# One 512-column run for both halves of the tokens in the projections of a two-block kernel

## The chip, the cores and the metric

One core of a Trainium2 chip runs the whole program. The metric is device time in microseconds (us), the median of several executions; lower is better. The engines are named as in the profile: PE (TensorE, with PEld for its weight loads), DVE (VectorE), ACT (ScalarE), POOL (GpSimd) and SP, which issues the transfers of the weights. PSUM is the memory into which PE accumulates; a tile of 128 x 512 fp32 values fills one of its banks.

## What is computed

A block with two layers runs first, then a second block, on 256 tokens of width 1024. The change touches only the first block:

```python
for l in range(DEPTH):                       # DEPTH = 2
    x = layer_norm(ALPHA * x + 0.5 * swiglu(x, ffn_w1[l, 0], ffn_w2[l, 0]), ...)
    x = layer_norm(ALPHA * x + hybrid_mixer(x, ...), ...)
    x = layer_norm(ALPHA * x + 0.5 * swiglu(x, ffn_w1[l, 1], ffn_w2[l, 1]), ...)

def swiglu(x, w1, w2):                       # D_FF = 2816
    g, u = jnp.split(x @ w1, 2, axis=-1)
    return (jax.nn.silu(g) * u) @ w2

def hybrid_mixer(x, w_in, ...):
    b_gate, c_gate, v, x_r, y_r, g_logits = jnp.split(x @ w_in, SPLITS, axis=-1)
    y_a = (b_gate * causal_depthwise_conv(c_gate * v, sc_w, 3)) @ w_out_conv
    xc = causal_depthwise_conv(x_r, rc_w, 4) + rc_b
    gates = sigmoid(per-head products of xc with rg_w)
    h = rg_lru(xc, gates[0], gates[1], a_param)          # a scan over the tokens
    y_b = (h * jax.nn.gelu(y_r)) @ w_out_rnn
    g_a, g_b = jnp.split(sigmoid(g_logits + b_merge), 2, axis=-1)
    return (g_a * y_a + g_b * y_b) @ w_o
```

## The kernel before

All products run on PE with fp32r operands, and the fp32 precision is kept by splitting each operand into a high part (rounded to fp32r) and a low part (the rest). A product is then three matmuls: high weight with high token, high weight with low token, low weight with high token.

**Weights.** `Weights` streams all weights in a fixed order as blocks of 1 MB; half of a block (128 x 1024) is the unit here, and it is called a weight half. `pump` splits a weight half: ACT casts it to the high part (L195), DVE subtracts that from the raw values for the low part (L196). Six split halves are held, so splits run some five halves ahead of PE. Every engine runs its instructions in the order in which the program wrote them, so where `pump`, `done` or `spend` stand in the code sets what ACT and DVE have ahead of them.

**Projections with the weights stationary.** `ws` (L314) takes one weight half, with 8 slices of 128 x 128, and for each slice k loads the high weights twice and the low weights once; each load is followed by a run of 256 columns (L317 with the high tokens, L318 with the low tokens, L319 again with the high tokens). All add into the same 256 columns of a PSUM tile. `group` does this for two halves and so fills one tile of 512 columns. The tokens are in `xT`, `za` or `hg`, laid out as [high/low, k, token].

**PSUM.** `mm_tile` hands out four tiles in turn (two of the pool `mm`, two of `mmo`). A tile can be written again only when those who read it are done: four tiles later.

**The feed-forward network** (`ffn`). The first two of 22 pairs of weight halves are done in another form (`begin`, `finish`, L334). Then 20 calls of `pair(p)`: two halves of w1 in `group`, SiLU by ACT (L534), the product with the other half by DVE (L536), the split of the result `ht` (L311 by ACT, L312 by DVE). In the first pair `turn_early` transposes the results of the first two halves and splits them into `ht` as well. After pair p (up to p = 18) the down projection `ts` runs for pair p - 2 (L370: twelve matmuls of 512 columns); it reads the split `ht` of that pair.

**The mixer** (`mixer`). Two groups of four slices each. In a group: projections Y and X in pairs of halves (Gelu by ACT, convolution by DVE, L649 and L651), then for each of four slices C and V (`c_gate * v` on DVE, L723, its convolution L725 and L727), the recurrent gates (L666 to L668), and per two slices two halves B, whose product with the convolution (L741) is split into `za` (L311, L312). The steps of the recurrence (`lru`, L678 to L703) are pieces that `done` puts between the others; they end with `hg`. Then eight steps of the output: two halves of gate logits (`gs`, L766), one half `woc` that reads all of `za`, one half `wor` that reads all of `hg` (in `merge`), and the down projection `wo`. After each stage a layer norm follows (`tail`, `ln_vec`, `to_xT`).

The rest of the kernel, from 1297 us on, is the second block; its own projections still go through `ws`.

Of the kernel before, what the change touches and what calls it, by code (L numbers as in the profile page):

```python
# [9 lines left out]
F32 = mybir.dt.float32  # L10
# [214 lines left out]
def kernel(ctx, tc, x, blocks, vecs, lnrows, consts, rows, bias_w, wr, out):  # L225
# [88 lines left out]
    def ws(ps, half, xT, mid=None):  # L314
        w = half.rearrange("p h (k c) -> p h k c", k=8)
        for k in range(8):
# [3 lines left out]
            if mid and k == 3:  # L320
                mid()

    def group(keys, xT, then=None, mid=None):
        ps = mm_tile()
        for q, key in enumerate(keys):
            half = W.take(*key)
            ws(ps[:, q * 256:q * 256 + 256], half, xT, mid)
            (then or done)()
        return ps
# [41 lines left out]
                                 start=(first and hx == 0 and hw == 0), stop=(last and hx == 1))  # L371

    def new_xT():
        return apool.tile([128, 2, 8, 256], F32R, tag="xT", name="xT")

    def to_xT(xT, src, T, new=mm_tile, mid=None):
        todo = []
# [130 lines left out]
    def ffn(l, j, xT, last):  # L508
# [12 lines left out]
        def pair(p):  # L521
            turn = [0]

            def then():
                W.release()
                turn[0] += 1
                if turn[0] == 1:
                    W.pump(1)
                    if p == 2:
                        turn_early()  # L530

            ps = group([("w1", l, j, p, 0), ("w1", l, j, p, 1)], xT, then)
            sl = p1.tile([128, 512], F32, tag="t512", bufs=3, name="sl")
            nc.scalar.activation(sl[:, 0:256], ps[:, 0:256], AF.Silu)  # L534
            h32 = p1.tile([128, 256], F32, tag="t256", bufs=4, name="h32")
            nc.vector.scalar_tensor_tensor(h32, ps[:, 256:512], 0.5, sl[:, 0:256], op0=ALU.mult, op1=ALU.mult)  # L536
            W.pump(1)
            ht = p1.tile([128, 2, 256], F32R, tag="h2k", bufs=8, name="ht")
            split_out(ht[:, 0], ht[:, 1], h32)
            hs[p] = ht  # L540
            c = ada_block(l, j, p)
            if c is not None:
                if p == 6:
                    nc.scalar.activation(cb, cb, AF.Silu)
                w = W.take("ada", c)
                nc.vector.scalar_tensor_tensor(junk, w, 1.0, cb, op0=ALU.mult, op1=ALU.mult, accum_out=modc[:, c:c + 1])
                W.release_raw()
            step(1.2)
# [49 lines left out]
    def mixer(l, xT):  # L598
        v0 = l * V_LAYER

        def col(o):
            return vec[:, v0 + o:v0 + o + 1]
# [17 lines left out]
                    nc.tensor.transpose(pts[i // 2][:, o:o + 128], ev[T][:, i * 128:i * 128 + 128], ident)  # L620
            return pts

        za = p1.tile([128, 2, 8, 256], F32R, tag="za", name="za")
        hg = p1.tile([128, 2, 8, 256], F32R, tag="hg", name="hg")
        for grp in range(2):
            b = 4 * grp
            gely = p1.tile([128, 4, 256], F32, tag="gely", name="gely")
# [3 lines left out]
            aa = p1.tile([128, 4, 256], F32, tag="grp4", name="aa")  # L631
            xch = {}
            for i in (0, 2):
                if b + i == 0:
                    ps, px = early()
                else:
                    ps = group([("in", l, OFF_YR, b + i + q) for q in range(2)], xT)
                nc.scalar.activation(gely[:, i:i + 2].rearrange("p a t -> p (a t)"), ps, AF.Gelu_apprx_tanh)
                ps = px if b + i == 0 else group([("in", l, OFF_XR, b + i + q) for q in range(2)], xT)
                xps = []  # L640
                for q in range(2):
                    xp = p1.tile([128, 260], F32, tag="xp", bufs=2, name="xp")
                    nc.vector.memset(xp[:, 0:3], 0.0)
                    nc.scalar.copy(xp[:, 3:259], ps[:, q * 256:q * 256 + 256])
                    xps.append(xp)
                for q in range(2):
                    f = b + i + q
                    xp, o = xps[q], xc[:, i + q]
                    nc.vector.tensor_scalar(o, xp[:, 0:256], col(V_RC + f), col(V_RCB + f), op0=ALU.mult, op1=ALU.add)  # L649
                    for t in range(1, 4):  # L650
                        nc.vector.scalar_tensor_tensor(o, xp[:, t:t + 256], col(V_RC + 8 * t + f), o, op0=ALU.mult, op1=ALU.add)  # L651
                    xh = p1.tile([128, 2, 256], F32R, tag="h2k", bufs=8, name="xch")
                    soon.append(lambda xh=xh, o=o: split_out(xh[:, 0], xh[:, 1], o))
                    xch[i + q] = xh
# [53 lines left out]
            for i in (0, 2):  # L708
                pcs = []
                for q in range(2):  # L710
                    f = b + i + q
                    ps = mm_tile()
                    h = W.take("in", l, OFF_C, f)
                    ws(ps[:, 0:256], h, xT)
                    done(1)
                    h = W.take("in", l, OFF_V, f)
                    ws(ps[:, 256:512], h, xT)
                    done(1)
                    cs = p1.tile([128, 256], F32, tag="t256", bufs=4, name="cs")
                    nc.scalar.copy(cs, ps[:, 0:256])  # L720
                    pc = p1.tile([128, 260], F32, tag="xp", bufs=2, name="pc")
                    nc.vector.memset(pc[:, 0:2], 0.0)
                    nc.vector.tensor_mul(pc[:, 2:258], ps[:, 256:512], cs)  # L723
                    cv = p1.tile([128, 256], F32, tag="t256", bufs=4, name="cv")
                    nc.vector.tensor_scalar(cv, pc[:, 0:256], col(V_SC + f), None, op0=ALU.mult)  # L725
                    for t in range(1, 3):
# [2 lines left out]
                    for hd in range(2):  # L729
                        if GATES[hd] == i + q:  # L730
                            gates(hd)
                            if hd:
                                bg.append(lru())
                ps = mm_tile()
                for q in range(2):
                    h = W.take("in", l, OFF_B, b + i + q)
                    ws(ps[:, q * 256:q * 256 + 256], h, xT)
                    done(1)
                for q in range(2):
                    f = b + i + q  # L740
                    nc.vector.tensor_mul(pcs[q], ps[:, q * 256:q * 256 + 256], pcs[q])  # L741
                    split_out(za[:, 0, f], za[:, 1, f], pcs[q])
        acc = new_acc()
        g = []
# [2 lines left out]
        held = {}  # L747

        def merge(i):
            ps, gs = held.pop(i)  # L750
            h = W.take("wor", l, i)
            ws(ps[:, 256:512], h, hg)
            done(1)
            m2 = p1.tile([128, 512], F32, tag="t512", bufs=3, name="m2")
            nc.vector.tensor_mul(m2, ps, gs)
            m1 = p1.tile([128, 256], F32, tag="t256", bufs=4, name="m1")
            nc.vector.tensor_add(m1, m2[:, 0:256], m2[:, 256:512])
            mt = p1.tile([128, 2, 256], F32R, tag="h2k", bufs=8, name="mt")
            split_out(mt[:, 0], mt[:, 1], m1)
            ms[i] = mt  # L760

        for i in range(8):
            ps = group([("in", l, OFF_G, 8 * q + i) for q in range(2)], xT)
            gs = p1.tile([128, 512], F32, tag="gs", bufs=2, name="gs")
            for q in range(2):
                nc.scalar.activation(gs[:, q * 256:q * 256 + 256], ps[:, q * 256:q * 256 + 256], AF.Sigmoid,  # L766
                                     bias=col(V_BM + 8 * q + i), scale=1.0)
            ps = mm_tile()
            h = W.take("woc", l, i)
            ws(ps[:, 0:256], h, za)  # L770
            done(1)
            held[i] = ps, gs
            if i == 1:
                flush()
            if i >= 1:
# [1022 lines left out]
```

## Time and profile before

| | us |
|---|---|
| median of 3 runs | 1801.39 (1798.95 to 1804.64) |
| the profiled execution | 1805.13 |
| its span, first to last instruction | 1803.3 |
| granted TensorE clock, mean | 0.984 |

| engine | busy us | share of the span |
|---|---|---|
| PE | 1741.4 | 97% |
| PEld | 1580.5 | 88% |
| DVE | 1286.3 | 71% |
| ACT | 975.8 | 54% |
| POOL | 62.1 | 3% |

By time: first feed-forward network to 212 us, first mixer to 459, second network to 652, third to 843, second mixer to 1090, fourth network to 1297, second block to the end. A busy PE in this profile is one whose runs overlap (a run of 256 columns is listed with 283 ns, while the next one starts 120 ns after it), so rates are to be read from the starts of the instructions and not from their lengths. The same holds in a smaller measure for DVE and ACT, whose listed times include a last part under which the next instruction already runs. The clock in the views is the share of full speed: 1.00 is 2.4 GHz, 0.50 is 1.2 GHz.

### The profile page before, as it was taken

How to read it: one execution, taken by the hardware profiler on the slowest of the kernel's cores; microseconds unless marked ns; L12 is line 12 of the kernel's file. 1: busy time of each engine (PE TensorE's matmuls, PEld its weight loads, DVE VectorE, ACT ScalarE, POOL GpSimd, SP SyncE). 2: the span in 40 equal slices, each digit the busy share in tenths (PEclk: the TensorE clock that was granted, in tenths of full speed). 3: DMA queues.
4: the chain of work that ended last, by engine and by line, in shares of the span. 5: the costliest groups of instructions: out<-in, count | busy, mean ns of one | idle time of the engine just before them, and what ended most of it. 6: DMA issues, size and time to landing. Idle time of an engine off the chain costs nothing. (4 is left out here: it accounts for less than half of the span.)

```text
span 1803.3 us, 27776 instructions
## 1 busy us (share of the span) xinstructions
PE 1741.4 (97%) x11369; PEld 1580.5 (88%) x11369; DVE 1286.3 (71%) x1753; ACT 975.8 (54%) x1340; POOL 62.1 (3%) x74
## 2 busy tenths in 40 slices
PE   7999999999999999999999998999899889999998
PEld 6999899999899989998999987899798677878776
DVE  5666878756666675668787566455778778998997
ACT  5444576644444444445666444344466547777775
POOL 0000000000000000000000000000024120000000
PEclk9999999999999999999999999999899989999999
DMA  8576554554656665666445545655352357989883
GB/s 319 203 258 240 234 183 169 191 207 146 238 209 238 255 246 186 251 241 236 188 165 195 202 150 226 210 188 184 114 187 88 130 195 277 350 312 343 338 319 138
DMA packets 56391, 394.26 MB, mean 219 GB/s; under 512 B 6424, under 2 KB 6728, under 8 KB 9920
## 3 DMA queue, kind: packets, MB, share of 16 engines
q1 hardware_dynamic: 52416, 375.94, 56.3%
q0 software_dynamic: 3264, 15.74, 2.5%
q8 instruction: 91, 1.49, 0.3%
q10 hardware_dynamic: 576, 0.74, 0.1%
q14 instruction: 44, 0.36, 0.1%
HBM read 391.30 MB, written 3.19 MB: 219 GB/s over the span
## 5 line engine op out<-in xcount | busy, mean ns | idle before, releaser
L196 DVE TENSOR_TENSOR split<-raw,split 128x1024 fp32r<-128x1024 f32 x611 | 735.8, 1224 | 302.7 <-ACT split L195 300.3
L195 ACT CAST split<-raw 128x1024 fp32r<-128x1024 f32 x611 | 628.2, 1048 | 252.5 <-PE mmo L319 70.4
L317 PE MATMUL mm<-xT,split 128*128 128x256 f32 x1208 | 342.0, 283 | 0.0
L319 PE MATMUL mm<-xT,split 128*128 128x256 f32 x1208 | 341.9, 283 | 0.0
L318 PE MATMUL mm<-xT,split 128*128 128x256 f32 x1208 | 341.8, 283 | 0.0
L317 PE MATMUL mmo<-xT,split 128*128 128x256 f32 x1008 | 285.5, 283 | 0.0
L319 PE MATMUL mmo<-xT,split 128*128 128x256 f32 x1008 | 285.2, 283 | 0.0
L318 PE MATMUL mmo<-xT,split 128*128 128x256 f32 x1008 | 285.2, 283 | 0.0
L317 PEld LDWEIGHTS mm<-xT,split 128*128 128x128 f32 x1208 | 231.7, 192 | 1.6
L318 PEld LDWEIGHTS mm<-xT,split 128*128 128x128 f32 x1208 | 231.7, 192 | 1.6
L319 PEld LDWEIGHTS mm<-xT,split 128*128 128x128 f32 x1208 | 231.7, 192 | 0.0
L370 PE MATMUL acc<-split,ht 128*128 128x512 f32 x816 | 200.1, 394 | 0.0
L317 PEld LDWEIGHTS mmo<-xT,split 128*128 128x128 f32 x1008 | 193.4, 192 | 1.4
L318 PEld LDWEIGHTS mmo<-xT,split 128*128 128x128 f32 x1008 | 193.3, 192 | 1.4
L319 PEld LDWEIGHTS mmo<-xT,split 128*128 128x128 f32 x1008 | 193.3, 192 | 0.0
L1527 PE MATMUL hp<-split,xg 128*128 128x512 f32 x768 | 187.7, 398 | 0.8 <-DVE split L196 0.8
L370 PEld LDWEIGHTS acc<-split,ht 128*128 128x128 f32 x816 | 150.5, 190 | 30.3 <-issue 1.7
L1527 PEld LDWEIGHTS hp<-split,xg 128*128 128x128 f32 x768 | 143.0, 188 | 34.7 <-DVE split L196 1.1
L1585 PE MATMUL y<-split,ht 128*128 128x512 f32 x360 | 87.2, 397 | 0.0
L1585 PEld LDWEIGHTS y<-split,ht 128*128 128x128 f32 x360 | 67.1, 188 | 15.8
L196 DVE TENSOR_TENSOR split<-spare,split 128x1024 fp32r<-128x1024 f32 x54 | 65.6, 1223 | 7.6 <-ACT split L195 7.1
L195 ACT CAST split<-spare 128x1024 fp32r<-128x1024 f32 x54 | 56.1, 1052 | 14.5 <-PE hp L1527 7.5
(454 smaller groups left out, 2115.9 us busy)
## 6 DMA issues: line engine op xcount, KB each, us to landing
raw<-in_w_dram SPq DMA_DIRECT2D x328, 1024.0 KB, 4.8
spare<-in_w_dram SPq DMA_DIRECT2D x27, 1024.0 KB, 4.8
lng<-in_ln_dram POOLq DMA_DIRECT2D x6, 1024.0 KB, 4.9
raw<-in_w_dram SPq DMA_DIRECT2D x4, 512.0 KB, 10.4
scr<-brow POOLq DMA_DIRECT2D x1, 2048.0 KB, 8.2
cb<-in_row_dram POOLq DMA_DIRECT2D x3, 512.0 KB, 5.6
norm<-mrow POOLq DMA_DIRECT2D x2, 512.0 KB, 6.3
braw<-scr POOLq DMA_DIRECT2D x2, 512.0 KB, 4.7
```

The costliest lines, as they stand in the source:

```text
L195: self.nc.scalar.copy(t[:, 0], r)
L196: self.nc.vector.tensor_sub(t[:, 1], r, t[:, 0].bitcast(F32))
L317: nc.tensor.matmul(ps, w[:, 0, k], xT[:, 0, k], start=(k == 0), stop=False)
L318: nc.tensor.matmul(ps, w[:, 0, k], xT[:, 1, k], start=False, stop=False)
L319: nc.tensor.matmul(ps, w[:, 1, k], xT[:, 0, k], start=False, stop=(k == 7))
L370: nc.tensor.matmul(acc[T][n], a[:, hx], half[:, hw, n * 512:n * 512 + 512], start=(first and hx == 0 and hw == 0), stop=(last and hx == 1))
L1527: nc.tensor.matmul(ps, xgs[g][:, hx, k], wv[:, hw, kk], start=(k == 0 and hx == 0 and hw == 0), stop=(k == 7 and hx == 1))
L1585: nc.tensor.matmul(ys[g][n][:, 0:w], ht[:, hx, q], half[:, hw, o:o + w], start=(j == 0 and q == 0 and hx == 0 and hw == 0), stop=(j == 3 a ...
```

## The change

The tokens are laid out as [k, high/low, token], so that the 256 high and the 256 low values of a slice stand side by side. `wide` takes the place of `ws` in the feed-forward networks and in all of the mixer's projections with stationary weights: for each slice the high weights are loaded once and 512 columns run (high and low tokens) into both parts of a tile; then the low weights are loaded and 256 columns (high tokens) run into the second part. The slices are taken from the last to the first. The two parts of the tile have to be added: `join` copies the second part to SBUF by ACT and adds the first part to it by DVE. A weight half now has a PSUM tile of its own. What read the PSUM tile before reads the joined result in SBUF.

```diff
+    def wide(key, xT):
+        half, ps = W.take(*key), mm_tile()
+        w = half.rearrange("p h (k c) -> p h k c", k=8)
+        both = ps.rearrange("p (h t) -> p h t", h=2)
+        for i in range(8):
+            k = 7 - i
+            nc.tensor.matmul(both, w[:, 0, k], xT[:, :, k], start=(i == 0), stop=False)
+            nc.tensor.matmul(ps[:, 256:512], w[:, 1, k], xT[:, 0, k], start=False, stop=(i == 7))
+        return ps
+
+    def join(dst, ps):
+        nc.scalar.copy(dst, ps[:, 256:512])
+        nc.vector.tensor_add(dst, ps[:, 0:256], dst)
...
-        return apool.tile([128, 2, 8, 256], F32R, tag="xT", name="xT")
+        return apool.tile([128, 8, 2, 256], F32R, tag="xT", name="xT").rearrange("p k h t -> p h k t")
...
-            ps = group([("w1", l, j, p, 0), ("w1", l, j, p, 1)], xT, then)
             sl = p1.tile([128, 512], F32, tag="t512", bufs=3, name="sl")
-            nc.scalar.activation(sl[:, 0:256], ps[:, 0:256], AF.Silu)
+            for q in range(2):
+                join(sl[:, q * 256:q * 256 + 256], wide(("w1", l, j, p, q), xT))
+                if q == 0:
+                    nc.scalar.activation(sl[:, 0:256], sl[:, 0:256], AF.Silu)
+                then()
             h32 = p1.tile([128, 256], F32, tag="t256", bufs=4, name="h32")
-            nc.vector.scalar_tensor_tensor(h32, ps[:, 256:512], 0.5, sl[:, 0:256], op0=ALU.mult, op1=ALU.mult)
+            nc.vector.scalar_tensor_tensor(h32, sl[:, 256:512], 0.5, sl[:, 0:256], op0=ALU.mult, op1=ALU.mult)
...
-                    ps = mm_tile()
-                    h = W.take("in", l, OFF_C, f)
-                    ws(ps[:, 0:256], h, xT)
+                    cs = p1.tile([128, 256], F32, tag="t256", bufs=4, name="cs")
+                    join(cs, wide(("in", l, OFF_C, f), xT))
                     done(1)
-                    h = W.take("in", l, OFF_V, f)
-                    ws(ps[:, 256:512], h, xT)
-                    done(1)
-                    cs = p1.tile([128, 256], F32, tag="t256", bufs=4, name="cs")
-                    nc.scalar.copy(cs, ps[:, 0:256])
                     pc = p1.tile([128, 260], F32, tag="xp", bufs=2, name="pc")
                     nc.vector.memset(pc[:, 0:2], 0.0)
-                    nc.vector.tensor_mul(pc[:, 2:258], ps[:, 256:512], cs)
+                    join(pc[:, 2:258], wide(("in", l, OFF_V, f), xT))
+                    done(1)
+                    nc.vector.tensor_mul(pc[:, 2:258], pc[:, 2:258], cs)
...
-                ps = mm_tile()
-                for q in range(2):
-                    h = W.take("in", l, OFF_B, b + i + q)
-                    ws(ps[:, q * 256:q * 256 + 256], h, xT)
-                    done(1)
                 for q in range(2):
                     f = b + i + q
-                    nc.vector.tensor_mul(pcs[q], ps[:, q * 256:q * 256 + 256], pcs[q])
+                    bt = p1.tile([128, 260], F32, tag="xp", bufs=2, name="bt")
+                    join(bt[:, 0:256], wide(("in", l, OFF_B, f), xT))
+                    done(1)
+                    nc.vector.tensor_mul(pcs[q], bt[:, 0:256], pcs[q])
                     split_out(za[:, 0, f], za[:, 1, f], pcs[q])
```

Projections Y and X (all but the first two of each, which stay as they were), the gate logits, `woc` and `wor` are changed in the same way: `join(dst, wide(key, tokens))`, then `done()`, then the activation or product on the joined tile. `za` and `hg` get the new layout too.

How the change moves instructions is shown at two places. First DVE at the start of the third feed-forward network, from the product of the early halves (`sl`, first row) on; `ht` are the splits that the first down projection reads. Before:

```order
L558 SCALAR_TENSOR_TENSOR sl<-mm,sl 128x256
L196 TENSOR_TENSOR split<-raw,split 128x1024 x3
L312 TENSOR_TENSOR ht<-mm,ht 128x256 x2
L536 SCALAR_TENSOR_TENSOR h_6641<-mmo,sl 128x256
L196 TENSOR_TENSOR split<-raw,split 128x1024
L312 TENSOR_TENSOR ht<-h_6641,ht 128x256
```

And with the change:

```order
L575 SCALAR_TENSOR_TENSOR sl<-mm,sl 128x256
L196 TENSOR_TENSOR split<-raw,split 128x1024 x2
L335 TENSOR_TENSOR sl<-mmo,sl 128x256
L196 TENSOR_TENSOR split<-raw,split 128x1024
L312 TENSOR_TENSOR ht<-mm,ht 128x256 x2
L335 TENSOR_TENSOR sl<-mmo,sl 128x256
L553 SCALAR_TENSOR_TENSOR h_5813<-sl 128x256
L196 TENSOR_TENSOR split<-raw,split 128x1024
L312 TENSOR_TENSOR ht<-h_5813,ht 128x256
```

The sum of the first half (L335) now stands ahead of the third split and of both `ht`. On ACT the same three stand in this order: its copy, the SiLU (which reads the sum), the cast of the third split, the two casts of `ht`.

Second, DVE in the first mixer, around the last two halves B of the second group: `gi`, `xc` and `gely` belong to the recurrence, `cv` is the convolution, `bt` the joined B. Before:

```order
L196 TENSOR_TENSOR split<-raw,split 128x1024
L698 TENSOR_TENSOR gi<-gi,gr 128x1024
L196 TENSOR_TENSOR split<-raw,split 128x1024
L701 SCALAR_TENSOR_TENSOR xc<-aa,gi 128x256 x3
L741 TENSOR_TENSOR cv<-mmo,cv 128x256
L312 TENSOR_TENSOR za<-cv,za 128x256
L741 TENSOR_TENSOR cv<-mmo,cv 128x256
L312 TENSOR_TENSOR za<-cv,za 128x256
L196 TENSOR_TENSOR split<-raw,split 128x1024
```

And with the change:

```order
L335 TENSOR_TENSOR bt<-mm,bt 128x256
L196 TENSOR_TENSOR split<-raw,split 128x1024
L723 TENSOR_TENSOR gi<-gi,gr 128x1024
L760 TENSOR_TENSOR cv<-bt,cv 128x256
L312 TENSOR_TENSOR za<-cv,za 128x256
L335 TENSOR_TENSOR bt<-mmo,bt 128x256
L196 TENSOR_TENSOR split<-raw,split 128x1024
L726 SCALAR_TENSOR_TENSOR xc<-aa,gi 128x256 x3
L760 TENSOR_TENSOR cv<-bt,cv 128x256
L312 TENSOR_TENSOR za<-cv,za 128x256
L335 TENSOR_TENSOR gs<-mm,gs 128x256
L196 TENSOR_TENSOR split<-raw,split 128x1024
```

Each of the two products now follows its own sum, and the first `za` no longer stands behind the scan (L726); the last `za` still does, with two sums more ahead of it.

## Rows read from the trace of the kernel before

**Rows 1.** Page, part 1: busy us, share of the span, instructions.

```profile
PE 1741.4 (97%) x11369; PEld 1580.5 (88%) x11369; DVE 1286.3 (71%) x1753; ACT 975.8 (54%) x1340; POOL 62.1 (3%) x74
```

**Rows 2.** Windows: length; busy PE, PEld, DVE, ACT, POOL; clock, DMA share, GB/s.

```profile
27.00:212.00 185.00, 183.25 (x1265) 170.61 (x1263) 128.00 (x191) 84.99 (x119) 0.00 (x0) 1.00 0.63 234
212.00:459.00 247.00, 243.78 (x1891) 236.48 (x1892) 178.36 (x259) 139.34 (x203) 0.71 (x2) 0.99 0.51 184
```

**Rows 3.** Waits of PE in 212 to 459 us: us in total, times, longest.

```profile
PE mm L334 <- DVE xT L382: 2.5, 1, 2.5
```

**Rows 4.** Timeline, PEld: start, us; loads for runs of 512 columns.

```profile
21.23 1.32 PEld L334 LDWEIGHTS mmo<-split,xT 128*128 128x128 f32 x6
...
22.59 1.32 PEld L334 LDWEIGHTS mm<-split,xT 128*128 128x128 f32 x6
```

**Rows 5.** Timeline, PE, the end of one pair and the next down projection.

```profile
100.96 0.28 PE L319 MATMUL mm<-xT,split 128*128 128x256 f32 x1
101.08 2.91 PE L370 MATMUL acc<-split,ht 128*128 128x512 f32 x12
103.83 0.28 PE L317 MATMUL mmo<-xT,split 128*128 128x256 f32 x1
```

**Rows 6.** Groups by line: count | busy us, mean ns | idle before, releaser.

```profile
L720 ACT COPY cs<-mmo 128x256 f32<-128x256 f32 x8 | 2.9, 362 | 12.7 <-PE mmo L319 12.7
...
L723 DVE TENSOR_TENSOR pc<-mmo,cs 128x256 f32<-128x256 f32 x8 | 3.4, 422 | 1.2 <-ACT cs L720 1.2
```

**Rows 7.** Windows: one pair and its down projection, 9 us.

```profile
100.00:109.00 9.00, 9.00 (x67) 8.51 (x66) 5.99 (x8) 3.73 (x5) 0.00 (x0) 1.00 0.63 228
```

**Rows 8.** Timeline, PE, ACT and DVE at the third network's start.

```profile
657.42 0.28 PE L317 MATMUL mmo<-xT,split 128*128 128x256 f32 x1
658.39 3.15 ACT L195 CAST split<-raw 128x1024 fp32r<-128x1024 f32 x3
660.28 3.49 DVE L196 TENSOR_TENSOR split<-raw,split 128x1024 fp32r<-128x1024 f32 x3
661.44 0.37 ACT L311 CAST ht<-mm 128x256 fp32r<-128x256 f32 x1
663.60 2.91 PE L370 MATMUL acc<-split,ht 128*128 128x512 f32 x12
663.68 0.42 DVE L312 TENSOR_TENSOR ht<-mm,ht 128x256 fp32r<-128x256 f32 x1
```

**Rows 9.** Windows: first mixer, from C and V of slice 2 to slice 5.

```profile
261.53:307.53 46.00, 46.00 (x386) 46.00 (x385) 41.91 (x72) 27.45 (x38) 0.00 (x0) 1.00 0.51 183
```

**Rows 10.** Timeline, PE and DVE where that stretch begins.

```profile
259.82 0.28 PE L317 MATMUL mm<-xT,split 128*128 128x256 f32 x1
261.53 0.42 DVE L723 TENSOR_TENSOR pc<-mmo,cs 128x256 f32<-128x256 f32 x1
```

**Rows 11.** Timeline, DVE: a small instruction and the one behind it.

```profile
226.07 0.42 DVE L312 TENSOR_TENSOR xch<-xc,xch 128x256 fp32r<-128x256 f32 x1
226.41 1.22 DVE L196 TENSOR_TENSOR split<-raw,split 128x1024 fp32r<-128x1024 f32 x1
```

**Rows 12.** Timeline, PE and DVE around the first `woc` of the first mixer.

```profile
334.70 0.28 PE L317 MATMUL mm<-xT,split 128*128 128x256 f32 x1
339.17 0.42 DVE L312 TENSOR_TENSOR za<-cv,za 128x256 fp32r<-128x256 f32 x1 [0.47 <-ACT za L311]
340.40 0.42 DVE L312 TENSOR_TENSOR za<-cv,za 128x256 fp32r<-128x256 f32 x1 [0.47 <-ACT za L311]
340.46 0.28 PE L317 MATMUL mmo<-za,split 128*128 128x256 f32 x1
```

**Rows 13.** Waits of PE in 1283 to 1290 us.

```profile
PE mm L387 <- DVE xn L501: 4.4, 1, 4.4
```

**Rows 14.** Windows right behind the waits of rows 3 and 13; clock third from the end.

```profile
454.00:458.00 4.00, 4.00 (x12) 3.10 (x11) 3.50 (x8) 0.30 (x1) 0.00 (x0) 0.57 0.32 133
...
1287.00:1294.00 7.00, 5.43 (x17) 4.43 (x18) 6.03 (x14) 1.76 (x4) 0.00 (x0) 0.53 0.47 194
```

More of the change, by code (lines that the diff above doesn't have):

```diff
@@ L633, in mixer @@
             for i in (0, 2):
+                gv = gely[:, i:i + 2].rearrange("p a t -> p (a t)")
                 if b + i == 0:
                     ps, px = early()
+                    nc.scalar.activation(gv, ps, AF.Gelu_apprx_tanh)
                 else:
-                    ps = group([("in", l, OFF_YR, b + i + q) for q in range(2)], xT)
-                nc.scalar.activation(gely[:, i:i + 2].rearrange("p a t -> p (a t)"), ps, AF.Gelu_apprx_tanh)
-                ps = px if b + i == 0 else group([("in", l, OFF_XR, b + i + q) for q in range(2)], xT)
+                    yr = p1.tile([128, 512], F32, tag="t512", bufs=3, name="yr")
+                    for q in range(2):
+                        join(yr[:, q * 256:q * 256 + 256], wide(("in", l, OFF_YR, b + i + q), xT))
+                        done()
+                    nc.scalar.activation(gv, yr, AF.Gelu_apprx_tanh)
                 xps = []
@@ L643, in mixer @@
                     nc.vector.memset(xp[:, 0:3], 0.0)
-                    nc.scalar.copy(xp[:, 3:259], ps[:, q * 256:q * 256 + 256])
+                    if b + i == 0:
+                        nc.scalar.copy(xp[:, 3:259], px[:, q * 256:q * 256 + 256])
+                    else:
+                        join(xp[:, 3:259], wide(("in", l, OFF_XR, b + i + q), xT))
+                        done()
                     xps.append(xp)
@@ L749, in merge @@
         def merge(i):
-            ps, gs = held.pop(i)
-            h = W.take("wor", l, i)
-            ws(ps[:, 256:512], h, hg)
+            m2, gs = held.pop(i)
+            join(m2[:, 256:512], wide(("wor", l, i), hg))
             done(1)
-            m2 = p1.tile([128, 512], F32, tag="t512", bufs=3, name="m2")
-            nc.vector.tensor_mul(m2, ps, gs)
+            nc.vector.tensor_mul(m2, m2, gs)
             m1 = p1.tile([128, 256], F32, tag="t256", bufs=4, name="m1")
@@ L762, in mixer @@
         for i in range(8):
-            ps = group([("in", l, OFF_G, 8 * q + i) for q in range(2)], xT)
             gs = p1.tile([128, 512], F32, tag="gs", bufs=2, name="gs")
             for q in range(2):
[L766 to L770, printed above, removed]
+                gq = gs[:, q * 256:q * 256 + 256]
+                join(gq, wide(("in", l, OFF_G, 8 * q + i), xT))
+                done()
+                nc.scalar.activation(gq, gq, AF.Sigmoid, bias=col(V_BM + 8 * q + i), scale=1.0)
+            m2 = p1.tile([128, 512], F32, tag="t512", bufs=3, name="m2")
+            join(m2[:, 0:256], wide(("woc", l, i), za))
             done(1)
-            held[i] = ps, gs
+            held[i] = m2, gs
             if i == 1:
```

4 lines of the change are left out of this document (2 added, 2 removed).

## The prediction

> **What bounds the kernel now.** First the page's busy shares: PE 97%, DVE 71%, ACT 54% [rows 1]. Shares are averages, so the stages come next: in the first network PE is busy for 183.25 of 185.00 us, in the first mixer for 243.78 of 247.00 [rows 2]. The list of waits then says how often PE stood still: the longest wait in the whole first mixer is 2.5 us, for the transposed tokens after a layer norm [rows 3]. So up to 1297 us time is the number of PE's runs times their spacing. The DMA share of 0.51 to 0.63 [rows 2] leaves the weights out of it. The spacing is read from starts. A run of 256 columns is followed by the next after 100.96 to 101.08 = 0.120 us [rows 5]; at 2.4 GHz the columns alone are 0.1067, so 0.0133 us belong to the change of weights. Six runs of 512 columns, each behind a load of its own, take 22.59 - 21.23 = 1.36, or 0.2267 each [rows 4]: again 0.0133 over their 0.2133. The twelve runs of a down projection take 103.83 - 101.08 = 2.75, or 0.229 each [rows 5].
>
> **What the change saves on PE.** Columns stay the same; of three loads and runs per slice two are left. A slice took 3 x 0.120 = 0.360 us, and will take 0.2267 + 0.120 = 0.3467: 0.0133 less, 0.107 for the 8 slices of a weight half (2.773 in place of 2.880). Halves that change: 4 networks x 20 pairs x 2 = 160; per mixer 12 (Y, X) + 16 (C, V) + 8 (B) + 16 (gate logits) + 8 + 8 (`woc`, `wor`) = 68, twice 136. Together 296 x 0.107 = **31.6 us**. With 0.229 for the long run it would be 296 x 8 x 0.011 = 26; that is the lower end.
>
> The Trainium skill speaks against this (page "TensorE: Matmul & The Clock Gate", section "Back-to-back issue gap"): it puts a run at its columns plus 2.5 ns, so that a run taken away would be worth 2.5 ns and the whole saving would be about 6 us, an estimate from that figure. The rows measure 13 ns at both lengths, and I go by them.
>
> **What it adds: 296 copies on ACT and 296 sums on DVE.** The nearest rows: an ACT copy of 256 columns out of PSUM is 0.36 us, a DVE product of a PSUM and an SBUF tile 0.42 [rows 6]. The next DVE instruction starts 0.34 us after such a small one [rows 11], so back to back a sum costs 0.34 to 0.42. On ACT 28 older copies (C, X) fall away. Totals: DVE about 296 x 0.42 = 124, ACT 268 x 0.36 = 96. Whether they cost time is decided stage by stage.
>
> *Networks, steady state: nothing.* In 9 us (a pair and its projection) DVE is busy 5.99 and ACT 3.73 [rows 7]; two joins add 0.8 and 0.7, while PE needs 5.55 + 2.75 = 8.30 per pair. The results are read two pairs later, and a bank two pairs later too. If this cover failed by 0.1 us per pair, it would cost 8 us over 80 pairs.
>
> *Networks, start: a new wait, about 1.5 us each.* The first down projection stood at 663.60 and reads the high part of `ht`, cast at 661.44; the low part, from 663.68, is needed only by its fifth matmul [rows 8], 4 x 0.2267 = 0.9 us later. Now the first join stands ahead. Its sum comes after two splits on DVE: 660.28 + 2 x 1.13 = 662.55, done at 662.97 (1.13 is the spacing of the three splits up to 663.68 [rows 8]). ACT, which has to run the SiLU on that sum before anything else, then needs 0.3 for it, 1.0 for the cast of the next split and 0.37 for `ht`: about 664.6. PE, 0.2 earlier, would be there at 663.4 and waits 1.2; DVE's split and low part end near 665.9, against 665.5 when the fifth matmul is due: 0.4 more. In the two networks behind a mixer I find 1.3. Four times 1.5 = **6 us** (0 if the SiLU gets through earlier, 10 if each takes one more split).
>
> *Mixers, between the two groups: about 4 us each.* From slice 2 to slice 5 DVE is busy 41.91 of 46.00 us [rows 9], because the recurrence runs there. In this stretch fall 16 sums: 41.91 + 16 x 0.34 = 47.4, while PE's 46.00 shrink by 16 x 0.107 to 44.3. DVE so falls 3.1 us behind even with no idle time at all, and 7.2 if it keeps its 4.1 us of idle time (the 0.47 of [rows 12] are such: `za` waits for ACT, ACT for the product). What allows for that is the ring of four banks. A bank used to hold two halves; now it holds one, and has to be free three halves, 8.3 us, after it was filled. Where gates run (two banks in one half's time), the sum of C of slice 5 must be done 2.77 + 2.88 = 5.65 us after its last run. The product of slice 2 begins 261.53 - 259.82 = 1.7 us behind PE [rows 10]; with one sum and a copy ahead it will be about 2.4. Then 2.4 + 3.1 to 7.2 = 5.5 to 9.6 stands against 5.3 allowed: a wait of 0.2 to 4.3. Followed in order, ACT's part in each join keeps the idle time up, so I take 4, near the upper end. It shows as waits of PE for L335. Twice: **8 us** (0 to 14).
>
> *Mixers, first `woc`: about 4 us each.* It reads all of `za`. The last `za` started at 340.40, that is 340.40 + 0.42 - 334.70 = 6.1 us after PE left the last B; `woc` began at 340.46, two halves (5.76) after it [rows 12], and, as it takes the slices upward, used that `za` only at 340.46 + 7 x 0.36 = 342.98. That is 2.2 us to spare. Now the slices run downward, so it is needed at once, 5.55 us after the last B. And it comes later: the sums of eight halves since the gates, when DVE was level with PE, are 8 x 0.34 = 2.7, one more trip to ACT and back 0.5 to 1. That gives 6.1 + 3.5 = 9.6 against 5.55: **4 us** twice, **8 us** (4 to 12; no less than 4, because 2.5 us of it come from the turned order alone).
>
> *The clock behind these waits: 5 us.* After PE's wait of 2.5 us [rows 3] the granted clock is 0.57 from 454 to 458, after that of 4.4 us [rows 13] 0.53 from 1287 to 1294 [rows 14], that is mostly 1.2 GHz: 4 x 0.43 = 1.7 and 7 x 0.47 = 3.3 us of full speed lost. The wait of 4 us at `woc` lies between them, so 2.5 each, twice 5 (0 to 13, should the waits between the groups do it too).
>
> Everything else (layer norms, the other projections, the second block) issues the same instructions: no cost.
>
> **Sum:** -31.6 + 6 + 8 + 8 + 5 = -4.6 us. The profiled execution took 1805.13 us, so 1800.5 in that state; against the median of 1801.39 it is 1796.8, or **1797**. A measurement of this kernel can tell a change over 0.3% (5.4 us) from none, so the forecast is: no change that can be told, with the gain of PE spent on waits.
>
> **Rivals.**
> *DVE and ACT keep up.* All waits but the four starts vanish: -31.6 + 6, some 1776, down to 1770 without those. For it: DVE's average load in the mixer, 178.36 of 247 [rows 2], has room for 68 x 0.34 = 23 us. Against it: the stretch of [rows 9], which lies above its share, and the turned order. In between, half of the waits: 1797 - 13 = 1784.
> *DVE becomes the bound of the mixers: slower.* If every sum waits for its copy as `za` waits for ACT (0.47 us [rows 12]), the 16 sums of the stretch add 16 x 0.47 = 7.5 us, and a like amount before `woc`. The two waits then grow from 4 to some 8 and 9 us, with both followed by the low clock (3.3 each): -31.6 + 6 + 2 x (8 + 9 + 6.6) = +21.6, some 1823. It decides from about 0.15 us of waiting per sum on; below that the sum stays under zero.
> *Runs of 512 columns save only 2.5 ns each,* by the page above: -6 + 27 = +21, 1822. The spacing in [rows 4] and [rows 5] speaks against it.
> That the change does not do what it says is no case: the program's order has the 2368 long and 2368 short runs.
>
> **How the numbers follow.** The forecast (within 0.3%): 0.36. Half of the waits or fewer: 0.31, and no waits of the mixers at all: 0.10; these two are faster, 0.41. DVE as bound, in full or in part: 0.20, and the small saving: 0.03; slower, 0.23. The likeliest case alone spans 1796 to 1807. The range leaves out about one in ten on each side: below, most of the case without waits (1780 keeps half of the waits); above, the full case of the DVE bound (1811 keeps its first half).
>
> **What would show it.** Right: runs of 512 and 256 columns spaced 0.227 and 0.120; PE's waits for `ht` at four starts of 1 to 2 us; waits of PE for L335 before the gates of the second group, and one of about 4 us for `za` before the first `woc`, in each mixer; lower clock behind it; DVE busy near 1410. Wrong: PE's busy share in the mixers still 0.99 (then the first rival), waits in every group and in steady pairs (then the second), or a spacing of 0.23 and more for the long runs.

## The result: 1.2% slower, and the profile after

| | before | with the change |
|---|---|---|
| median, us | 1800.56 (1798.95 to 1804.64, 4 runs) | 1822.49 (1821.90 to 1825.31, 4 runs) |
| the profiled execution, us | 1805.13 | 1821.9 |
| its span, us | 1803.3 | 1820.0 |

The ratio is 1.0119, interval 1.0107 to 1.0132: some 22 us slower, where 1797 and a range up to 1811 were forecast. The profiled execution of before was itself 4.6 us above its median, so between the two traces there are only 16.8 us to find.

Page, part 1, and windows of the changed kernel (columns as in [rows 2]):

```profile
PE 1731.0 (95%) x9001; PEld 1454.0 (80%) x9001; DVE 1390.9 (76%) x2049; ACT 1072.6 (59%) x1608; POOL 62.2 (3%) x74
```

```profile
27.00:212.00 185.00, 181.85 (x947) 153.66 (x945) 141.17 (x231) 99.69 (x158) 0.00 (x0) 1.00 0.64 235
212.00:470.00 258.00, 246.18 (x1346) 210.57 (x1345) 203.88 (x327) 157.38 (x257) 0.53 (x1) 0.97 0.49 176
...
345.00:352.00 7.00, 4.81 (x15) 4.16 (x16) 6.04 (x10) 5.67 (x9) 0.00 (x0) 0.53 0.41 150
...
451.00:455.00 4.00, 4.00 (x12) 3.14 (x11) 2.88 (x5) 0.24 (x2) 0.00 (x0) 0.57 0.73 262
```

Against [rows 1] PE has 2368 runs fewer, DVE 296 instructions and 105 us more. The loss has a place: from the start of DVE's last instruction of one layer norm (L421, now L435) to that of the next, the first mixer took 457.77 - 211.39 = 246.4 us and takes 257.8; the second 246.4 and 257.5, together 22.6 longer. The four networks come out 0.2 longer to 2.4 shorter, together 3.4 shorter. The second block, whose program is the same, is 2.5 shorter. In a mixer PE was busy for 99% of the time [rows 2], now for 246 of 258 us. It has new waits in four places. The list of its waits in the changed kernel, whole run (columns as in [rows 3]):

```profile
PE mm L329 <- DVE za L312: 8.9, 2, 4.4
...
PE acc L384 <- ACT ht L311: 3.1, 4, 1.0
PE acc L450 <- ACT split L195: 2.9, 2, 1.5
...
PE mm L330 <- DVE split L196: 2.1, 4, 0.6
...
PE mm L330 <- DVE xp L664: 1.5, 2, 0.8
PE acc L450 <- DVE split L196: 1.5, 2, 0.8
...
PE mm L691 <- DVE cs L335: 1.3, 2, 0.8
...
PE mmo L330 <- DVE split L196: 0.5, 2, 0.2
```

From the top: the first `woc` waits for `za` (8.9); the four first down projections for `ht` (3.1); the ends of the mixers, where `wo` is finished, for the split of the last weight half (2.9 + 1.5); and, between the two groups of a mixer, the rest (5.4, for weight splits, `xp` and a sum). Together 21.8 us.

**Where za is lost.** Timeline of DVE and of PE (start, us, engine, line, out<-in) in the changed kernel:

```profile
341.96 0.42 DVE L335 TENSOR_TENSOR bt<-mmo,bt 128x256 f32<-128x256 f32 x1
342.84 1.23 DVE L196 TENSOR_TENSOR split<-raw,split 128x1024 fp32r<-128x1024 f32 x1 [0.46 <-ACT split L195]
343.98 1.85 DVE L726 TENSOR_TENSOR_SCAN xc<-aa,gi 128x256 f32<-128x256 f32 x3
345.74 0.40 DVE L760 TENSOR_TENSOR cv<-bt,cv 128x256 f32<-128x256 f32 x1
346.62 0.43 DVE L312 TENSOR_TENSOR za<-cv,za 128x256 fp32r<-128x256 f32 x1 [0.47 <-ACT za L311]
```

```profile
336.93 0.40 PE L329 MATMUL mm<-xT,split 128*128 128x512 f32 x1
...
342.47 0.28 PE L330 MATMUL mmo<-xT,split 128*128 128x256 f32 x1
347.19 0.76 PE L329 MATMUL mm<-za,split 128*128 128x512 f32 x1 [4.43 <-DVE za L312]
```

PE left the last half B at 336.93, where the next half begins. The last sum of B starts 5.0 us later and is done at 342.4; then a weight split and three scans, 2.9 us, stand ahead of the product that reads it. `za` is complete 10.1 us after PE left B, where it was 6.1 before [rows 12]. Behind this wait the window 345 to 352 above has the clock at 0.53; before, in the same window, nothing waited:

```profile
345.00:352.00 7.00, 7.00 (x62) 7.00 (x60) 5.13 (x5) 6.97 (x10) 0.00 (x0) 1.00 0.44 150
```

**The end of the mixer.** The last run of the last `wor` half on PE, then the cast of the last merge (`mt`) and the weight cast behind it on ACT, first before, then with the change:

```profile
434.18 0.28 PE L319 MATMUL mmo<-hg,split 128*128 128x256 f32 x1
436.56 0.41 ACT L311 CAST mt<-m 128x256 fp32r<-128x256 f32 x1 [2.35 <-DVE m L757]
```

```profile
442.33 0.28 PE L330 MATMUL mmo<-hg,split 128*128 128x256 f32 x1
447.48 0.40 ACT L311 CAST mt<-m 128x256 fp32r<-128x256 f32 x1 [2.35 <-DVE m L774]
447.79 1.04 ACT L195 CAST split<-raw 128x1024 fp32r<-128x1024 f32 x1
```

From the listed end of that run to the cast it is 4.9 us in place of 2.1.

**What a run costs.** Starts of weight halves on PE in the changed kernel (each row the first long run of a half), late in the first group and early in the mixer:

```profile
253.32 0.40 PE L329 MATMUL mm<-xT,split 128*128 128x512 f32 x1
...
256.15 0.40 PE L329 MATMUL mmo<-xT,split 128*128 128x512 f32 x1
```

```profile
225.28 0.39 PE L329 MATMUL mm<-xT,split 128*128 128x512 f32 x1
...
228.06 0.39 PE L329 MATMUL mmo<-xT,split 128*128 128x512 f32 x1
```

Seven halves early in each mixer take the forecast 2.77 to 2.78 us; nearly all others, those of the networks too, take 2.81 to 2.83. Of the 0.107 us that each half was to save about half is missing there.

### The profile page after: what moved, and what is told of

The parts are those of the page before. It is cut to its first block, busy times and chain, and to the rows that moved or that the text cites. A ratio compares the mean times of both kernels' runs of the same rounds, so it can differ in the third digit from the quotient of the medians.

```text
span 1820.0 us, 23834 instructions
## 1 busy us (share of the span) xinstructions
PE 1731.0 (95%) x9001; PEld 1454.0 (80%) x9001; DVE 1390.9 (76%) x2049; ACT 1072.6 (59%) x1608; POOL 62.2 (3%) x74
## 5 line engine op out<-in xcount | busy, mean ns | idle before, releaser
L329 PE MATMUL mm<-xT,split 128*128 128x512 f32 x1056 | 378.8, 398 | 0.2
L329 PE MATMUL mmo<-xT,split 128*128 128x512 f32 x1056 | 378.9, 398 | 0.0
L330 PE MATMUL mm<-xT,split 128*128 128x256 f32 x1056 | 296.8, 281 | 3.6 <-DVE split L196 2.1
L330 PE MATMUL mmo<-xT,split 128*128 128x256 f32 x1056 | 296.5, 281 | 0.5 <-DVE split L196 0.5
L329 PEld LDWEIGHTS mmo<-xT,split 128*128 128x128 f32 x1056 | 198.7, 188 | 48.6
L329 PEld LDWEIGHTS mm<-xT,split 128*128 128x128 f32 x1056 | 198.4, 188 | 48.7 <-ACT xch L311 0.7
L330 PEld LDWEIGHTS mm<-xT,split 128*128 128x128 f32 x1056 | 199.3, 189 | 7.5 <-DVE split L196 3.4
L330 PEld LDWEIGHTS mmo<-xT,split 128*128 128x128 f32 x1056 | 199.6, 189 | 2.1 <-DVE split L196 1.1
L334 ACT COPY sl<-mm 128x256 f32<-128x256 f32 x80 | 29.8, 373 | 95.6 <-PE mm L330 95.6
L550 ACT ACTIVATE sl<-sl 128x256 f32<-128x256 f32 x80 | 33.5, 419 | 59.0 <-DVE sl L335 59.0
L334 ACT COPY sl<-mmo 128x256 f32<-128x256 f32 x80 | 29.8, 373 | 63.2 <-PE mmo L330 63.2
L195 ACT CAST split<-spare 128x1024 fp32r<-128x1024 f32 x54 | 56.1, 1053 | 14.5 <-PE hp L1544 7.1
L335 DVE TENSOR_TENSOR sl<-mm,sl 128x256 f32<-128x256 f32 x80 | 33.7, 422 | 39.3 <-ACT sl L334 39.3
```

The costliest lines, as they stand in the source:

```text
L195: self.nc.scalar.copy(t[:, 0], r)
L329: nc.tensor.matmul(both, w[:, 0, k], xT[:, :, k], start=(i == 0), stop=False)
L330: nc.tensor.matmul(ps[:, 256:512], w[:, 1, k], xT[:, 0, k], start=False, stop=(i == 7))
L334: nc.scalar.copy(dst, ps[:, 256:512])
L335: nc.vector.tensor_add(dst, ps[:, 0:256], dst)
L550: nc.scalar.activation(sl[:, 0:256], sl[:, 0:256], AF.Silu)
```

## The experiments

Ratios are to the kernel before, with their 95% interval; differences in us are between medians. Beside the experiments the kernel before had medians from 1800.5 to 1802.3, so a difference of 2 us or less between two experiments tells nothing. The theory: three losses in the mixers (trips of each sum through ACT and DVE, `za` read at once, the end of the mixer), each partly followed by low clock, and a long run that is dearer behind a short one. Rivals: DVE's own time for the sums; the order of slices or of runs decides nothing.

**e1: networks only.** `pair` as in the change; the mixer's lines as before.

> Long runs and sums in the four networks alone; the mixers as before. Theory (the loss lies in the mixers, the networks gain a little): the four networks come out as in the changed kernel, whose layer norms end +0.2, -1.0, -0.2 and -2.4 us from those of before, and the mixers take their old 246.4 us: about 3.4 us faster than before, 1797 (1794 to 1800). A half in the networks takes 2.83 us, and each start still waits about 1 us for ht. Rival (the networks gain only because the slower mixers let the weight loads run ahead): no gain, 1800 to 1804.

Measured 1796.11 us, ratio 0.9974 (0.996 to 0.9987): the theory. The loss is in the mixers; the networks gain a quarter of a per cent.

**e2: long runs first, then the short ones.**

```diff
         for i in range(8):
             k = 7 - i
             nc.tensor.matmul(both, w[:, 0, k], xT[:, :, k], start=(i == 0), stop=False)
+        for i in range(8):
+            k = 7 - i
             nc.tensor.matmul(ps[:, 256:512], w[:, 1, k], xT[:, 0, k], start=False, stop=(i == 7))
```

> The changed kernel, but in each half the eight long runs first, then the eight short ones. Theory (the long run is 10 ns dearer than in the projections because long and short alternate): long runs 0.227 to 0.229 and short ones 0.120 apart, a half takes 2.77 to 2.80 us in place of 2.83; 296 halves x 0.03 to 0.055 = 9 to 16 us less, 1806 to 1813. Rival (it lies in what the runs read, whatever their order): long runs stay at 0.233 or more, a half at 2.83, and the time at 1822.

Measured 1817.57, 1.0088 (1.0071 to 1.0105). PE's timeline in e2 (L329 long, L332 short runs):

```profile
253.12 2.00 PE L329 MATMUL mm<-xT,split 128*128 128x512 f32 x8
254.96 1.11 PE L332 MATMUL mm<-xT,split 128*128 128x256 f32 x8
255.91 2.00 PE L329 MATMUL mmo<-xT,split 128*128 128x512 f32 x8
```

A half takes 2.79 us. The eight long runs take 1.84, 0.230 each, the short ones 0.95. Within a block the trace has 233, 236, 228, 233, 231 ns from start to start and then 226 to 227: the first five long runs behind short ones are dearer. Where the two alternate, each long run is such a one. So the theory holds for the spacing, though not everywhere: the halves early in a mixer, above, alternate too and take 2.77. The time missed its forecast (1806 to 1813). Blocks save 0.035 us per half, and about half of that came through to the end (4.9 of 296 x 0.035 = 10.4 us). In the two traces it came through in the networks only: the mixers of e2 take 257.6 and 257.8 us, as in the changed kernel.

**e3: slices upward** (`k = i` in place of `k = 7 - i`).

> The changed kernel, but every half takes its slices upward (0 to 7). Theory (the turned order makes PE need the last za at once): the wait of 4.4 us at the first woc of each mixer shrinks by 7 slices of 0.353 us to about 2.0, and stands inside that half instead of ahead of it; the clock behind it falls for a shorter time or not at all (0 to 3.3 us): 5 to 11 us less in all, 1811 to 1817. Rival (the order of the slices decides nothing, DVE is late by as much anyway): waits of 4 us stay, 1820 to 1824.

Measured 1816.04, 1.0079 (1.0062 to 1.0095), 6.4 us less. PE's waits in e3, whole run:

```profile
PE mm L329 <- DVE za L312: 3.7, 2, 1.9
```

8.9 has become 3.7, and the clock stays at 1.00 behind it (344 to 352 us). The theory.

**e4: weight casts ahead of the joins.** In the networks `then()`, which pumps, stands ahead of `join`; in the mixers the pump does, in all of their joins (the cut shows C):

```diff
-                    join(cs, wide(("in", l, OFF_C, f), xT))
-                    done(1)
+                    ps = wide(("in", l, OFF_C, f), xT)
+                    W.release(1)
+                    W.pump(1)
+                    join(cs, ps)
+                    done(0)
```

> The changed kernel, but in every half the cast and split of a coming weight half are issued ahead of the join, not behind it (in the networks also the transposes and casts of the first two pairs). Theory (the joins wait for PE and hold the weight casts up behind them): the waits for the last wo weights at the mixers' ends (1.5 and 0.8 us) and the low clock behind them (1.7) go, and the starts of the networks wait 0.5 us less each: 8 to 11 us less, 1811 to 1815. Rival (a join that comes 1.0 us later frees its bank later): the waits between the groups and ahead of woc grow by 1 to 3 us in each mixer, and the time stays at 1820 to 1826.

Measured 1812.13, 1.0055 (1.0037 to 1.0073), 10.4 us less, but only one of the two reasons given holds. The networks no longer wait for `ht`, and in the two traces they are 7.4 us shorter. In the first mixer of e4 the waits change their names:

```profile
PE mm L329 <- DVE za L312: 3.5, 1, 3.5
...
PE mm L698 <- DVE pc L751: 1.9, 1, 1.9
PE mm L329 <- DVE xp L668: 1.0, 1, 1.0
PE acc L450 <- ACT split L195: 1.0, 1, 1.0
PE mm L329 <- DVE yr L335: 0.9, 1, 0.9
PE acc L450 <- DVE split L196: 0.8, 1, 0.8
```

A sum that comes later makes PE wait between the groups (the rival), and the wait at the end hardly shrinks. Both mixers stay at 257 to 259 us.

**e5: no trip.** A join is one instruction of DVE, which reads PSUM as the sum did; columns 256 to 511 are left out.

```diff
-        nc.scalar.copy(dst, ps[:, 256:512])
-        nc.vector.tensor_add(dst, ps[:, 0:256], dst)
+        nc.vector.tensor_copy(dst, ps[:, 0:256])
```

> The changed kernel, but a join is one DVE copy of columns 0 to 255; the copy on ACT and the sum with columns 256 to 511 are left out, so the low products are missing from the output. Theory (the trip from PE to ACT and on to DVE in each join makes PE wait in the mixers): the waits between the groups (3.2 us in each mixer) fall under 1, those at the mixers' ends (2.6) under 0.5, the wait ahead of the first woc from 4.6 to 2 to 2.5, where only the turned order is left, the starts of the networks lose half of theirs; with the clock behind them 16 to 22 us less, 1800 to 1806. Rival (DVE's own time for the sums makes it late): DVE keeps almost all of its work, the waits lose less than a third, 1816 to 1819.

Measured 1803.86, 1.0014 (1.0002 to 1.0026), as the theory had it. First one group of e5, then the one of the changed kernel that it replaces (columns as in [rows 6]):

```profile
L334 DVE COPY sl<-mm 128x256 f32<-128x256 f32 x80 | 33.7, 421 | 22.5 <-PE mm L330 22.2
```

```profile
L335 DVE TENSOR_TENSOR sl<-mm,sl 128x256 f32<-128x256 f32 x80 | 33.7, 422 | 39.3 <-ACT sl L334 39.3
```

PE's waits in the first mixer of e5:

```profile
PE mm L329 <- DVE za L312: 2.7, 1, 2.7
...
PE acc L449 <- DVE split L196: 0.8, 1, 0.8
PE mm L330 <- DVE split L196: 0.4, 1, 0.4
```

DVE works as long per join (421 against 422 ns) and the mixers lose 2.8 and 1.2 us instead of 11.5 and 11.1. DVE's time for the sums is not the cause; the step on ACT is. Whether by its own 0.37 us or by its place in ACT's queue e5 doesn't tell, as it takes both away. One part of the theory failed: the starts of the networks were to lose half of their waits, and over the whole run they keep them (3.1 before this edit):

```profile
PE acc L383 <- ACT ht L311: 3.5, 4, 1.0
```

There the order of the casts decides (e4, e9). (Both operands of the sum cannot come out of PSUM: the Trainium skill, page "PSUM — Partial Sum Buffer", section "Specifications (TRN2)", allows a VectorE instruction one tensor input from there. No run here shows it.)

**e11: the last weight cast first.** `done(1, pump=2 if i == 7 else 1)` in `merge`.

> The changed kernel, but in the last merge of each mixer two weight halves are cast and split at once, so that the last wo half stands ahead of the cast of mt on ACT. Theory (that cast comes late because it stands behind mt, which waits for the longer chain of the merge): the wait of 1.6 us for the cast at the end of each mixer goes, the one of 1.0 for the split at least halves, and with the clock behind them 4 to 8 us are won: 1814 to 1818. Rival (mt itself is late then, or the raw weights): the wait stays with another name, 1820 to 1823.

Measured 1818.27, 1.0083 (1.0065 to 1.0102), 4.2 us less, at the edge of the forecast. At the first mixer's end:

```profile
PE acc L450 <- ACT mt L311: 1.6, 1, 1.6
```

Rival and theory share it: the cast and its split no longer hold PE up (1.5 and 0.8), but the merge itself is now what comes last, 1.6.

**e12: the first `woc` later.** The weights' order and the loop put it behind the second pair of gate logits (the cut shows the loop):

```diff
...
+            late[i] = gs
+            if i == 0:
+                continue
+            for k in sorted(late):
+                m2 = p1.tile([128, 512], F32, tag="t512", bufs=3, name="m2")
+                join(m2[:, 0:256], wide(("woc", l, k), za))
+                done(1)
+                held[k] = m2, late.pop(k)
...
```

> The changed kernel, but in each mixer the first woc half comes behind the second pair of gate logits and not ahead of it (the weights are laid out in that order too). Theory (PE's wait for za and the low clock behind it are the price of reading za at once): the wait of 4.6 us goes, with it the 2.4 to 2.8 us of low clock, 14 us in two mixers: 1807 to 1811. Rival (DVE is behind in any case, and PE waits for the sums of the gate logits or the merges instead): 1816 to 1822.

Measured 1811.39, 1.0053 (1.0035 to 1.007), 11.1 us less, just short of the forecast. The wait for `za` is gone, and with it the low clock in the same window:

```profile
345.00:352.00 7.00, 6.51 (x37) 5.40 (x35) 6.03 (x10) 5.57 (x8) 0.00 (x0) 1.00 0.43 150
```

**e13: readers right behind their joins.** For V and B the product (and `split_out` of `za`) moves ahead of `done(1)`.

> The changed kernel, but for V and B the product that reads a sum (for B also the cast and rest of za) is issued right behind the join, ahead of the weight cast, the weight split and the recurrence's steps that followed it. Theory (za is late because the split of 1.2 us and scans of 1.9 stand between the last sum and its product): za comes 1.5 to 3 us earlier, the wait of 4.6 ahead of the first woc shrinks by as much, twice 2 to 3 us with less low clock behind it: 4 to 9 us less, 1813 to 1818. Rival (the trip itself is what is long; the order behind the join only says who waits): waits of PE for weight splits or sums between the groups grow by what za gains, 1820 to 1824.

Measured 1819.86, 1.0104 (1.0079 to 1.013): 2.6 us less, under the forecast 4 to 9, and as the two intervals overlap not clear of noise. The wait did shrink as expected:

```profile
PE mm L329 <- DVE za L312: 2.2, 1, 2.2
```

The mixers became 1.2 and 2.8 us shorter, but in the profiled execution the fourth network and the part behind it, where e13 changes nothing, took 2.3 and 1.8 longer. Most of that is the clock, which is 0.57 from 1145 to 1153 and from 1459 to 1467 us; in the trace of the changed kernel it is low for half as long in the first place and not at all in the second. The same network takes from 199.8 (e1) to 207.7 us (e13) in the traces with this program, so such differences say nothing of the edit. Three edits, each alone, take about half of the wait of 4.4 at `za`: upward slices leave 1.9, no trip 2.7, readers first 2.2. It has no single cause.

**e9, e7 and e10: the networks mended.** All three take the mixers as before. e9 is e1 with `then()` ahead of `join`; e7 adds the blocks of e2, and e10 runs the short block upward. (In e2, e3, e6 to e8, e10 and e14 the same products are summed in another order than in the change.)

> As e7 (wide runs in the networks alone, casts of weights and first pairs ahead of the join), but long and short runs alternate as in the change. Theory (the two gains of e7 are separate): a half takes 2.83 us in place of 2.79, 160 x 0.035 = 5.6 us over e7, 1791, and the networks start without a wait. Rival (e7 owes its gain to the order of the runs alone): 1795 to 1797, no better than e1.

> Wide runs in the networks alone (mixers as before), long runs first, then the short ones, and the casts of weights and first pairs ahead of the join. Theory (in the networks the saving stands once the starts wait for nothing): e1 gave 4.6 us; 160 halves x 0.035 = 5.6 and four starts x 1.3 = 5 come to it: 15 us faster than before, 1783 to 1790. Rival (what PE saves in a network is spent ahead of its layer norm or behind it, in the wait for the transposed tokens and the clock): no better than e1, 1793 to 1797.

> As e7, but the eight short runs take the slices upward while the long ones go downward. Theory (only the number of changes between long and short counts for the spacing): no difference to e7, 1783 to 1788. Rival (the order of the operands plays a part): a half differs from 2.79 us by over 0.02, and the time by over 3 us.

Measured: e9 1790.38, 0.9926 (0.9905 to 0.9947); e7 1785.35, 0.9918 (0.9894 to 0.9942); e10 1785.27, 0.9901 (0.9882 to 0.9921). The theories hold: the third network takes 191.3 us before, 189.1 in e9, 187.5 in e10. In e10 a pair with its projection takes 671.03 - 662.73 = 8.30 us, without a wait:

```profile
662.73 2.91 PE L385 MATMUL acc<-split,ht 128*128 128x512 f32 x12
...
671.03 2.91 PE L385 MATMUL acc<-split,ht 128*128 128x512 f32 x12
```

**e8: e7 and the gate logits.**

> As e7, and also the 16 halves of gate logits in each mixer in wide runs, with the cast ahead of the join. Theory (in this stretch DVE has room, and nothing of PE's waits for the sigmoids soon): 32 halves x 0.085 = 2.7 us under e7. Rival (the sums put the merges back, and the ends of the mixers wait for the last wo weights as in the changed kernel, 2.6 us and the clock, 1.7, each): 3 to 6 us over e7.

Measured 1784.73, 0.9908 (0.9885 to 0.9931): no difference to e7 that can be told. Neither case: 16 halves x 0.085 = 1.4 us saved in a mixer are spent in a new wait there:

```profile
PE mm L329 <- DVE gs L337: 1.4, 1, 1.4
```

**e6 and e14: everything wide, and mended.** e6 has the blocks, slices upward and the networks of e9; e14 the blocks, the networks of e10, and e11 to e13.

> The changed kernel with three mends at once: long runs first and then the short ones, slices upward, and in the networks the casts of weights and first pairs ahead of the join. Theory (each takes another loss away): e2 gave 4.9 us, e3 6.4, the networks' part of e4 about 6, together 17: 1804 to 1808, still not under the kernel before, as the waits between the groups and at the mixers' ends stay. Rival (the clock falls behind the next wait instead, or one mend uncovers another wait): 1809 to 1813.

> All projections wide as in the change, with every mend: long runs first, casts ahead in the networks, the first woc behind the second pair of gate logits, the last cast first, readers right behind their joins. Theory (the losses are separate): 1822.5 less 4.9 (e2), 5.7 (e9 against e1), 11.1 (e12), 4.2 (e11) and 0 to 5 for the readers: 1791 to 1797, better than before but not than e10, because the trips between the groups and at the mixers' ends still cost more than the mixers' 136 halves x 0.09 save. Rival (without PE's waits the mixers too become faster than before): under 1785.

Measured: e6 1801.38, 1.0001 (0.999 to 1.0012), better than forecast; e14 1796.42, 0.9981 (0.9967 to 0.9995), as forecast. PE's waits in the first mixer of e14, without the one for `xT`:

```profile
PE acc L452 <- ACT mt L312: 1.7, 1, 1.7
PE mm L694 <- DVE cs L337: 1.4, 1, 1.4
PE mm L330 <- ACT xch L312: 1.1, 1, 1.1
PE mm L330 <- ACT split L196: 0.8, 1, 0.8
PE mm L330 <- DVE yr L337: 0.4, 1, 0.4
PE mm L330 <- DVE gs L337: 0.4, 1, 0.4
```

These waits alone are 5.8 us, as much as 68 halves x 0.085 save; each mixer takes 250.4 us against 246.4 before, and PE is idle in it for 9.8 us against 3.3. With these mends together the mixers still lose (the casts ahead in the mixers, of e4, and the slices upward, of e3, are not among them), so as far as is measured the change is worth making in the networks alone, as in e10, which beats both kernels.

## Why the prediction was wrong

- **The step that failed first: "A slice [...] will take 0.2267 + 0.120".** 0.2267 came from long runs behind long runs [rows 4]; here each stands behind a short one. The 0.229 of [rows 5], where the first five of twelve are dearer, was read as the same thing, only worse measured, and 26 us taken for the lower end. Measured are some 2.83 us per half, in which a long run takes 0.232 to 0.241 (the prediction had named 0.23 and more as a sign of being wrong): 296 x 0.053 = 16 saved in place of 31.6. e2 shows that the order of long and short runs matters. It does not show the whole cause, since early in a mixer the same order costs the forecast 2.77; what decides between the two stays open. The rule weighed there (the Trainium skill, page "TensorE: Matmul & The Clock Gate", section "Back-to-back issue gap"), which the page gives for a run in isolation and not for a stream of loads and runs, lies on the other side: 2.5 ns for a run taken away, where a slice in this trace got 6 to 7 shorter (2.88 - 2.83 us over 8).
- **The step that was missing: "Everything else [...]: no cost".** Downstream of the joins the cast of the last merge begins 4.9 us after the last `wor` half instead of 2.1, and the last `wo` half is cast behind it: 4.4 us of waits at the two ends. That cast stood behind `mt` on ACT before too, but nobody had to wait for it. In e11 its wait goes, and the longer merge itself is left.
- **The clock: 5 us, measured 7.1 in new places.** It is 0.50 from 347.2 to 352.2 us behind the first `woc` and 0.51 from 988 to 994 behind the second, 2.5 + 2.9 us of full speed lost, as forecast; 4 x 0.43 = 1.7 come behind the first mixer's end, a place not foreseen. e12 shows the first two. The difference between the two executions is smaller, because the trace of before has low clock in places where the other has it for half as long or not at all (0.54 from 1082 to 1089, 0.57 from 1126 to 1134, 0.53 from 1287 to 1294 [rows 14], 0.57 from 1444 to 1452): the mean over the span is 0.984 in both.
- **First `woc`: right.** 8 forecast, 8.9 measured, `za` named, with the turned order in it (e3).
- **Between the groups: the size (8, measured 5.4), not the name.** The wait for L335 ahead of the gates is 1.3 of it; PE also waits for weight splits and for `xp`, which stand on DVE behind sums that wait for ACT.
- **Starts of the networks: right.** 6 forecast; 3.1 for the high part of `ht` and some 0.4 each for the low one. e9 gets them back.
- **Steady state of the networks: right,** no wait.

The sum with the measured terms: -16 + 4.7 + 5.4 + 8.9 + 4.4 + 7.1 = +14.5. It is to be set against the first block, which is 19.2 us longer between the two traces (22.6 - 3.4). So some 5 us stay open, and about as much again if the longer low clock that the trace of before has in the first block, from 1082 us on, is counted. Some 3 us are the ends of twenty waits: a run is listed with 0.28 us where the next is due after 0.12, so each wait costs 0.16 more than its listed time. The second block's 2.5 are the low clock of before from 1444 to 1452.

The rival with the sums as bound (1823) came to the right time by luck: its waits of 8 and 9 us in each mixer are 2.7 and 4.4, and its saving of 31.6 is 16. Its name is wrong too: DVE has the time (e5), it only gets its operand late.

## What to carry to other kernels

A run's price can depend on the runs ahead of it: read it where long and short runs alternate, or measure that. An extra eviction step costs its path (PE to ACT to DVE and on, each behind what its queue holds), not only the busy time that it adds: with the step on ACT gone and DVE as busy as before per join, little of the mixers' loss is left (e5). What PE saves in a stage whose other engines are late is spent on waits (e2, e8). Take such a change where results are needed late (the networks), and leave it where the next weights' readers are close. Then look at what the in-order queues have between a result and its reader, and issue weight casts ahead of instructions that wait for PE.

## What the runs showed of the hardware

In the changed kernel alternating runs of 512 and 256 columns settle in one of two rhythms, 693 ns for two slices (early in the mixers) or 1060 ns for three (from the first gates on, and nearly always in the networks), at a granted clock of 1.00 in both; after the waits around 940 us the faster one came back for three halves. What sets it stays open. The first five runs of 512 columns behind shorter ones take 1 to 9 ns more than the later ones (233, 236, 228, 233, 231 against 226 to 227), in the old kernel's down projections as well.
